# Moving a weight conversion behind a neighbourhood unit's normalising products on ScalarE

## The chip, the cores and the metric

The kernel runs on one core of one Trainium2 chip. The metric is device time in microseconds (us) of one execution; the median over the runs shown is compared. A profiled execution stands beside it, with its own time and with its span, which is the time from the first to the last instruction of the program. Engines are called TensorE (PE in the profile, PEld for its weight loads), VectorE (DVE), ScalarE (ACT), GpSimd (POOL) and SyncE (SP).

## The reference, cut to what matters

Two layers of a hybrid encoder on 512 tokens of width 1024. In each layer one projection feeds three mixers, which are merged by gates; a SwiGLU FFN and a gated input embedding follow. The mixer that the change touches is the 2-D neighbourhood attention: 8 heads, each query row sees a window of 8 x 16 neighbours, with a relative bias.

```python
proj = h @ w_in[i]
qa, ka, va, glu_in, qc, kc, vc, gates = jnp.split(proj, SPLITS, axis=-1)
ya = diff_attention(qa, ka, va, ...)
yb = conformer_conv(glu_in, ...)
yc = neighbourhood_attention(qc, kc, vc, rpb[i])
...
# neighbourhood_attention, one grid row at a time
s = jnp.einsum('bhwd,bhrwcd->bhwrc', q_r, kn).astype(jnp.float32) * scale
s = s + bias.transpose(0, 2, 1, 3)[None].astype(jnp.float32)
a = jax.nn.softmax(s.reshape(B, HC, GRID_W, KR * NA_KC), axis=-1)
...
return jnp.einsum('bhwrc,bhrwcd->bhwd', a, vn)
```

## The kernel before, in words

Activations lie transposed: 128 channels on the partitions, 512 tokens along the free dimension. Each float32 operand is held as two parts, a high one (rounded by a copy on ScalarE) and a low one (the rest, by a subtraction on VectorE), and a product is three matmuls on TensorE (`mm3`): high weights by high input, high weights by low input, low weights by high input. So the third matmul of a block is the first that needs the low part of the weights.

A block of weights of 128 x 1024 goes through `weights` (L189): a DMA into `wr`, a conversion on ScalarE into `wh` (the line of the helper is L145), and the subtraction on VectorE into `wl` (L159). Each of the three tags has 3 buffers. A block takes 24 matmuls (8 chunks of 3), and after every fourth chunk `tick` may put other work into the order of TensorE.

The order on TensorE is the order in which the program emits. The order on the other engines is made by a scheduler from priorities; the conversions of weights are put ahead by 400 places (`w_ahead`), so a conversion stands early in ScalarE's order, as soon as its buffers are free. `behind(i, then)` forces instruction `i` to stand after `then` in the order of their engine, with no wait beyond that.

A neighbourhood unit (`natten_unit`) is one head. There are 8 in a layer, called unit 0 to unit 7 here. Its first part emits the score matmuls for two halves (tiles `b` and `e`), a reduce with the bias added (L738, VectorE), four exponentials with their sums (ScalarE), a reciprocal for each half (L744, VectorE) and four normalising products on ScalarE (a copy with a scale, two for each half). Three ticks later TensorE transposes the four tiles (L754) and the result is split into `pt`, and two ticks after that the products with the values follow (L764).

The blocks of weights and the score matmuls of the units come in this order on TensorE in each layer. Q and K are the query and key blocks of neighbourhood pair 1 to 3, G and U the last gate and value blocks of the convolution's input, dQ and dK those of the differential attention's heads. dV is that mixer's value block; it is made by `values`, which converts on its own and does not go through `weights`.

| block on TensorE | units whose scores come in it or at its end |
|---|---|
| Q1 | unit 0 at its end |
| K1 | unit 1 at its end |
| G, Q2 | none (unit 0 is transposed in G, unit 1 in Q2) |
| K2 | unit 2 in its middle |
| U | unit 3 in its middle |
| Q3 | none |
| K3 | unit 4 in its middle |
| dQ0 | unit 5 in its middle |
| dK0 | none |
| dV | unit 6 in its middle, unit 7 at its end |
| dQ1, dK1, gatec 0 | none (unit 6 is transposed in dQ1, unit 7 in dK1) |

In the profile the conversions run in the order of the program. The name of a conversion tells the phase alone, so the blocks are told apart by counting: in layer 0 the conversions at 72.26, 77.47, 83.84, 91.16, 98.41 and 106.13 us are those of G, Q2, K2, U, Q3 and K3, and those at 155.79 and 156.74 us are dK1 and gatec 0.

A list `first_come` orders conversions already: `urgent` (for the splits of the transposed tiles) enters a count of 3, every call of `weights` takes one from each count in `gives_way`, and at zero the conversion of that call is put behind the entered split.

Of the kernel before, what the change touches and what calls it, by code (L numbers as in the profile page):

```python
# [14 lines left out]
AF = mybir.ActivationFunctionType  # L15
# [37 lines left out]
ORDER = (0, 2, 4, 6, 1, 3, 5, 7)  # L53
GAP = 144
AHEAD = 3
BACC = dict(dynamic_dma_scratch_size=1024)


# [4 lines left out]
class Net:  # L63
# [107 lines left out]
    def urgent(self, low):  # L171

        self.first_come.append([AHEAD, self.high, low])

    def gives_way(self, low):

        for u in self.first_come:
            u[0] -= 1
            if not u[0]:
                self.behind(self.high, u[1])  # L180
                self.behind(low, u[2])
        self.first_come = [u for u in self.first_come if u[0]]

    def weights(self, ap, n, then=None):
# [530 lines left out]
    def natten_unit(self, pr, u, st4, k2, st, y):  # L715

        nc, i = self.nc, self.i
        mm = nc.tensor.matmul
        head = 2 * pr + u
        bs = [self.sb(t, [P, 2, NW]) for t in ("b", "e")]  # L720
        with self.tc.high_priority(offset=100):
            for half, b in enumerate(bs):
                nc.sync.dma_start(b, self.a["bias"][i, head, half])
        m = self.sb("s", [P, 8])
        es = []
        for half, b in enumerate(bs):
            sc = self.ps("sc", (P, 2, NW))
            for t in range(2):
                qt = 2 * half + t
                keys = (lambda a, qt=qt: a[:, qt * P - P:qt * P + P]) if qt else \  # L730
                    (lambda a: a.rearrange("p (a b) -> p a b", b=P)[:, 0::3])
                self.scores(sc[:, t] if qt else sc[:, t].rearrange("p (a b) -> p a b", b=P),
                            st4, k2, u, slice(qt * P, (qt + 1) * P), keys, t == 0,
                            skip_group_check=True)
            for t in range(2):
                qt = 2 * half + t
                es.append(b[:, t])
                nc.vector.tensor_tensor_reduce(  # L738
                    out=b[:, t], in0=sc[:, t], in1=b[:, t], scale=-1.0, scalar=3.0e38,
                    op0=ALU.add, op1=ALU.min, accum_out=m[:, qt:qt + 1])  # L740
                self.act(b[:, t], b[:, t], AF.Exp, table="exp", scale=-1.0, bias=m[:, qt:qt + 1],
                         accum_out=m[:, 4 + qt:5 + qt])
            c = slice(4 + 2 * half, 6 + 2 * half)
            nc.vector.reciprocal(m[:, c], m[:, c])  # L744
            for t in range(2):
                self.act(b[:, t], b[:, t], AF.Copy, scale=m[:, c][:, t:t + 1])
        yield 3
        ps = []
        for half in range(2):
            pt = self.ps("tr", (P, 4, P))  # L750
            for n in range(4):
                kc, q = 2 * half + n // 2, (2 * half + (n + 1) // 2) % 4
                c = (kc != q - 1 if q else kc == 3) * P
                nc.tensor.transpose(pt[:, n], es[q][:, c:c + P], self.ident)  # L754
            pp = self.sb("pt", [P, 2, 512], F32R)
            self.urgent(self.split(pp[:, 0], pp[:, 1], pt.rearrange("p a b -> p (a b)")))
            ps.append(pp)
        yield 2
        av = self.ps(("av", "mm")[u])
        hc = (pr % 2) * 256 + u * P  # L760
        vs = st[pr // 2]
        for kc, (o, n, c) in enumerate(((0, 192, MOVE), (MOVE, 256, 256), (192, 256, 0), (320, 192, 256))):
            for k in range(2):
                mm(av[:, o:o + n], vs[kc // 2][:, kc % 2, hc:hc + P], ps[kc // 2][:, k, c:c + n],  # L764
                   start=kc == k == 0, stop=kc == 3 and k == 1, skip_group_check=True)
        rs, ro = (slice(0, 64), slice(64, P))[::-1 if u else 1]
        self.split(y[rs, 0], y[rs, 1], av[rs])
        self.tt(y[rs, 1], y[rs, 1].bitcast(F32), av[ro], ALU.add)
# [781 lines left out]
```

## Time and profile before

| | us |
|---|---|
| median of 3 runs | 1757.81 |
| lowest and highest | 1756.70 and 1757.99 |
| time of the profiled execution | 1756.33 |
| its span | 1754.6 |
| ScalarE busy | 965.5 |
| VectorE busy | 1427.1 |

The units of layer 0 lie at about 77 to 175 us of the span, those of layer 1 at about 946 to 1044 us. In the timeline each row has the start in us, the duration in us, the engine, the line, the operation with out<-in, and the count of instructions merged into the row; in brackets stands the idle time ahead of it and what ended it. On ScalarE and VectorE the next instruction starts about 0.1 us ahead of the end of the last.

### The profile page before, as it was taken

What the parts mean: (1) busy time and instruction counts of PE and PEld (TensorE: products, weight loads), DVE (VectorE), ACT (ScalarE), POOL (GpSimd) and SP (SyncE); (2) the same over time, 40 slices, a digit from 0 to 9 for tenths busy, and PEclk for the clock granted to TensorE, in tenths of its full rate; (3) what the DMA queues carried; (4) which work ended last, traced back from release to release, by engine and by line L of the source; (5) the groups of instructions that cost most, each with busy time, mean ns of one, the idle gap of its engine ahead of it and who ended that gap; (6) DMA issues with size and microseconds to landing.
All of it is one profiled execution on the core that took longest, in us unless ns stands there. A gap on an engine that the chain in (4) does not pass through costs nothing.

```text
span 1754.6 us, 24852 instructions
## 1 busy us (share of the span) xinstructions
PE 1747.0 (100%) x8842; PEld 1484.2 (85%) x8842; DVE 1427.1 (81%) x2371; ACT 965.5 (55%) x1737; POOL 104.0 (6%) x114
## 2 busy tenths in 40 slices
PE   9999999999999999999999999999999999999998
PEld 7888888888888888888888888888888988888887
DVE  7968987998799687797776789889887985977876
ACT  5576545226577275574545665553365763745654
POOL 0000000000121020100000000000001210201000
PEclk9999999999999999999999999999999999999999
DMA  6575641334757365543545755323256774755332
GB/s 227 162 193 157 165 123 49 108 99 141 232 160 185 120 169 157 143 120 127 158 130 165 202 141 158 105 73 96 93 178 197 184 171 121 181 143 155 96 107 95
DMA packets 114636, 253.81 MB, mean 145 GB/s; under 512 B 16848, under 2 KB 23504, under 8 KB 114512
## 3 DMA queue, kind: packets, MB, share of 16 engines
q1 hardware_dynamic: 101264, 228.10, 42.8%
q0 software_dynamic: 12672, 23.07, 7.9%
q8 instruction: 70, 1.15, 0.3%
q10 hardware_dynamic: 576, 1.05, 0.2%
q14 instruction: 54, 0.44, 0.1%
HBM read 215.46 MB, written 7.34 MB: 127 GB/s over the span
## 4 chain that ended last, share of the span: by engine, by line
PE 94%; DVE 2%; ACT 1%; DMA 1%; issue 1%; SPq 0%; POOL 0%; ACTq 0%; POOLq 0%; DVEq 0%
PE ffn_mm L1032 6%; PE ffn_sc L1032 6%; PE ffn_mm L196 4%; PE ffn_mm L197 4%; PE ffn_mm L198 4%; PE ffn_mm L1035 3%; PE ffn_sc L1035 3%; PE mergea_mm L198 2%; PE mergea_mm L196 2%; PE mergea_mm L197 2%; PE ffn_tr L1032 2%; PE diff_sc L819 2%; PE gatec_mm L197 2%; PE gatec_mm L196 2%; PE gatec_mm L198 2%; PE gateb_mm L198 2%
## 5 line engine op out<-in xcount | busy, mean ns | idle before, releaser
L162 DVE SCALAR_TENSOR_TENSOR conv_z<-glu_z,pre_par,conv_z 128x512 f32<-128x512 f32 x240 | 179.5, 748 | 3.4
L145 ACT ACTIVATE ffn_wh<-ffn_wr 128x1024 fp32r<-128x1024 f32 (+1 forms) x92 | 92.8, 1021 | 99.4 <-PE ffn_mm L197 70.0
L159 DVE TENSOR_TENSOR ffn_wl<-ffn_wr,ffn_wh 128x1024 fp32r<-128x1024 f32 (+1 forms) x92 | 107.1, 1175 | 21.0 <-ACT ffn_wh L145 20.5
L998 POOL DMA_DIRECT2D ffn_qk<-w_fu x88 | 78.0, 994 | 588.5 <-DMA ffn_qk<-w_fu 329.5
L145 ACT ACTIVATE mergea_wh<-mergea_wr 128x1024 fp32r<-128x1024 f32 (+1 forms) x32 | 27.1, 846 | 96.8 <-PE mergea_mm L197 79.6
L159 DVE TENSOR_TENSOR ffn_t<-ffn_mm,wo_rb 128x512 f32<-128x512 f32 (+1 forms) x46 | 31.1, 677 | 51.7 <-PE ffn_mm L198 51.7
L159 DVE TENSOR_TENSOR ffn_wl<-ffn_qk,ffn_wh 128x1024 fp32r<-128x1024 f32 x44 | 53.6, 1218 | 11.0 <-ACT ffn_wh L145 10.9
L145 ACT ACTIVATE diff_a<-diff_sc,diff_s 128x512 f32<-128x512 f32 x32 | 22.0, 689 | 72.9 <-DVE diff_s L912 72.9
L145 ACT ACTIVATE ffn_wh<-ffn_qk 128x1024 fp32r<-128x1024 f32 x44 | 46.7, 1062 | 26.8 <-PE ffn_mm L197 16.2
L196 PE MATMUL ffn_mm<-ffn_v,ffn_wh 128*128 128x512 f32 x132 | 51.4, 389 | 0.0
L197 PE MATMUL ffn_mm<-ffn_v,ffn_wh 128*128 128x512 f32 x132 | 51.4, 389 | 0.0
L198 PE MATMUL ffn_mm<-ffn_v,ffn_wl 128*128 128x512 f32 x132 | 51.3, 389 | 0.0
L196 PE MATMUL ffn_mm<-ffn_y,ffn_wh 128*128 128x512 f32 x132 | 51.3, 389 | 0.0
L197 PE MATMUL ffn_mm<-ffn_y,ffn_wh 128*128 128x512 f32 x132 | 51.3, 389 | 0.0
L198 PE MATMUL ffn_mm<-ffn_y,ffn_wl 128*128 128x512 f32 x132 | 51.3, 389 | 0.0
L145 ACT ACTIVATE natten_wh<-natten_wr 128x1024 fp32r<-128x1024 f32 x24 | 25.4, 1057 | 42.2 <-issue 15.2
L1032 PE MATMUL ffn_sc<-wo_h,ffn_wh 128*128 128x512 f32 x176 | 48.0, 394 | 0.0
L159 DVE TENSOR_TENSOR ffn_t<-ffn_t,ffn_e 128x256 f32<-128x256 f32 x84 | 46.2, 550 | 1.0 <-ACT ffn_e L145 0.9
L912 DVE TENSOR_REDUCE diff_s<-diff_sc 128x1 f32<-128x512 f32 x64 | 42.3, 683 | 3.7 <-PE diff_sc L819 3.6
L1032 PE MATMUL ffn_mm<-wo_h,ffn_wh 128*128 128x512 f32 x160 | 43.6, 394 | 0.0
L242 POOL TENSOR_TENSOR diff_rc<-diff_sm,pre_power 128x4 f32<-128x4 f32 x8 | 8.9, 1115 | 560.6 <-DVE diff_sm L162 560.6
L159 DVE TENSOR_TENSOR ffn_t<-ffn_t,ffn_t 128x512 f32<-128x512 f32 x44 | 30.2, 686 | 11.5 <-ACT ffn_t L145 11.5
(904 smaller groups left out, 5988.5 us busy)
## 6 DMA issues: line engine op xcount, KB each, us to landing
ffn_qk<-w_fu POOLq DMA_DIRECT2D x88, 256.0 KB, 6.7
ffn_wr<-w_fg SPq DMA_DIRECT2D x44, 512.0 KB, 4.2
ffn_wr<-w_fd SPq DMA_DIRECT2D x32, 448.0 KB, 4.0
ffn_r<-w_fu SPq DMA_DIRECT2D x44, 256.0 KB, 3.1
ffn_qk<-w_fg SPq DMA_DIRECT2D x44, 256.0 KB, 3.2
ffn_qk<-w_fu SPq DMA_DIRECT2D x44, 256.0 KB, 3.2
natten_wr<-w_in SPq DMA_DIRECT2D x16, 512.0 KB, 4.1
diff_wr<-w_in SPq DMA_DIRECT2D x16, 512.0 KB, 4.0
```

What stands on the lines that cost most here:

```text
L145: i = self.nc.scalar.activation(out, in_, func, **kw)
L159: return self.nc.vector.tensor_tensor(out, a, b, op)
L162: return self.nc.vector.scalar_tensor_tensor(out, a, s, b, op0, op1)
L196: mm(out, wh, ah, start=first, stop=False, **kw)
L197: mm(out, wh, al, start=False, stop=False, **kw)
L198: mm(out, wl, ah, start=False, stop=last, **kw)
L242: nc.gpsimd.tensor_tensor(col, ms, self.power, ALU.pow)
L819: self.nc.tensor.matmul(out, st4[:, u, qs], keys(st), start=first and n == 0, stop=n == 1, **kw)
L912: nc.vector.tensor_reduce(out=m[:, u:u + 1], in_=sc, op=ALU.max, axis=AX.X, negate=True)
L998: nc.gpsimd.dma_start(q, wu[:, lo], accum_op=ALU.add)
L1032: mm(out, wh[:, c], bs[k][b], start=first and k == 0, stop=False, skip_group_check=True)
L1035: mm(out[:, 0], wl[:, c], bs[k][b][:, 0], start=False, stop=k == 3, skip_group_check=True)
```

## The change

After the two normalising products of each half, the last of them is entered in `first_come` with a count of 2 and no partner on VectorE. So the conversion on ScalarE of the second call of `weights` that follows a unit is put behind the last normalising products of both halves of that unit. Nothing is computed otherwise, and no instruction is added or removed.

```diff
+ROWS_AHEAD = 2
...
             if not u[0]:
                 self.behind(self.high, u[1])
-                self.behind(low, u[2])
+                if u[2] is not None:
+                    self.behind(low, u[2])
...
             nc.vector.reciprocal(m[:, c], m[:, c])
             for t in range(2):
-                self.act(b[:, t], b[:, t], AF.Copy, scale=m[:, c][:, t:t + 1])
+                last = self.act(b[:, t], b[:, t], AF.Copy, scale=m[:, c][:, t:t + 1])
+            self.first_come.append([ROWS_AHEAD, last, None])
         yield 3
```

## The prediction

> **What bounds the kernel now.** I read the page first, parts 1 and 2, then the waits of TensorE, then its timeline and ScalarE's around the units.
>
> ```profile
> span 1754.6 us, 24852 instructions
> PE 1747.0 (100%) x8842; PEld 1484.2 (85%) x8842; DVE 1427.1 (81%) x2371; ACT 965.5 (55%) x1737; POOL 104.0 (6%) x114
> PEclk9999999999999999999999999999999999999999
> ```
>
> TensorE is busy all the time at a full granted clock. [...] So the room is in the waits, and there is hardly any:
>
> ```profile
> PE pre_av L348 <- DVE pre_zeror L421: 1.1, 1, 1.1
> PE natten_tr L754 <- ACT natten_e L145: 0.5, 2, 0.3
> ```
>
> The columns are total us, times, longest. The first is the start of the kernel. The second is what the change can touch: twice, once in each layer, the transposes of unit 6 wait for a normalising product. Matmul ends are modelled, so the loss is larger than the 0.5 us and is read from the starts (timeline of TensorE: unit 1's eight transposes undisturbed, then unit 6's in layer 0 and layer 1):
>
> ```profile
> 94.82 0.49 PE L754 MATMUL natten_tr<-pre_ident,natten_b 128*128 128x128 f32 x3
> ...
> 95.61 0.48 PE L196 MATMUL natten_mm<-glu_h,natten_wh 128*128 128x512 f32 x1
> ...
> 159.12 0.49 PE L754 MATMUL natten_tr<-pre_ident,natten_b 128*128 128x128 f32 x3
> 159.90 0.84 PE L754 MATMUL natten_tr<-pre_ident,natten_e 128*128 128x128 f32 x4 [0.29 <-ACT natten_e L145]
> ...
> 160.60 0.48 PE L196 MATMUL diff_mm<-glu_h,diff_wh 128*128 128x512 f32 x1
> ...
> 1027.90 0.49 PE L754 MATMUL natten_tr<-pre_ident,natten_b 128*128 128x128 f32 x3
> ...
> 1029.28 0.48 PE L196 MATMUL diff_mm<-ple_h,diff_wh 128*128 128x512 f32 x1
> ```
>
> Undisturbed they take 95.61 - 94.82 = 0.79 us; here 1.48 and 1.38 us. The loss is 0.69 + 0.59 = 1.28 us. That is all that this change can win on TensorE.
>
> **What the change moves.** It adds no instruction. But its count of 2 does not only reach the late unit. The second block behind units 0 to 4 is G, Q2, Q3, K3 and dK0; behind unit 5 it is dQ1; behind units 6 and 7 it is dK1, for both. A conversion now runs when its buffer comes free, two blocks ahead of its use, which is often before the unit's scores exist. After the change it waits for the unit's whole chain of reduce, exponentials, reciprocal and products. And since conversions keep the order of the program among themselves, the ones behind it (K2 behind Q2, gatec 0 behind dK1, dV behind dK0) move with it. The price is set by one comparison for each unit: the low part of the weights must be there when the block's third matmul (L198) is due.
>
> The step from the last product to that low part, from the rows of dK1 now (ScalarE, then VectorE):
>
> ```profile
> 155.79 1.04 ACT L145 ACTIVATE diff_wh<-diff_wr 128x1024 fp32r<-128x1024 f32 x1
> 156.74 1.05 ACT L145 ACTIVATE gatec_wh<-gatec_wr 128x1024 fp32r<-128x1024 f32 x1
> ...
> 163.40 0.90 ACT L145 ACTIVATE natten_e<-natten_e,natten_s 128x256 f32<-128x256 f32 x2
> ```
> ```profile
> 156.87 1.23 DVE L159 TENSOR_TENSOR diff_wl<-diff_wr,diff_wh 128x1024 fp32r<-128x1024 f32 x1 [0.82 <-ACT diff_wh L145]
> ```
>
> The conversion starts 0.10 us before the end of the one ahead (the 155.79 row ends at 156.83, the next starts at 156.74), takes 1.05, and the low part starts 0.04 us later and takes 1.23: 2.22 us from the end of the last product. One conversion that leaves the way shortens a chain behind it by its 0.95 us (156.74 - 155.79).
>
> *Units 6 and 7 to dK1, layer 0.* Now both conversions, dK1 and gatec 0, stand in the middle of unit 6's chain and delay units 6 and 7 by 2 x 0.95 = 1.90 us. Unit 7's last product ends at 164.30; with both gone, at 162.40. The low part of dK1 is ready at 164.62. dK1's third matmul is due at:
>
> ```profile
> 163.90 0.39 PE L198 MATMUL diff_mm<-glu_h,diff_wl 128*128 128x512 f32 x1
> ```
>
> So 164.62 - 163.90 = +0.72 us, net: that due time holds the 0.69 us of waiting that goes away, so TensorE really waits 1.41 us there and gets 0.69 back. The wait for unit 6 is replaced by a wait for dK1, with a longer one.
>
> *Unit 0 to G and unit 1 to Q2, layer 0.*
>
> ```profile
> 72.26 1.06 ACT L145 ACTIVATE glu_wh<-glu_wr 128x1024 fp32r<-128x1024 f32 x1 [0.34 <-PE natten_sc L705]
> ...
> 77.47 1.06 ACT L145 ACTIVATE natten_wh<-natten_wr 128x1024 fp32r<-128x1024 f32 x1 [1.06 <-PE natten_mm L197]
> ...
> 82.79 0.91 ACT L145 ACTIVATE natten_e<-natten_e,natten_s 128x256 f32<-128x256 f32 x2 [0.23 <-DVE natten_s L744]
> 83.84 1.06 ACT L145 ACTIVATE natten_wh<-natten_wr 128x1024 fp32r<-128x1024 f32 x1
> ...
> 89.31 0.90 ACT L145 ACTIVATE natten_e<-natten_e,natten_s 128x256 f32<-128x256 f32 x2
> ```
> ```profile
> 85.29 0.39 PE L198 MATMUL glu_mm<-glu_h,glu_wl 128*128 128x512 f32 x1
> ...
> 91.64 0.39 PE L198 MATMUL natten_mm<-glu_h,natten_wl 128*128 128x512 f32 x1
> ```
>
> G moves from 72.26 to behind unit 0. Q2 (77.47) leaves the front of that chain, so it ends at 83.70 - 0.95 = 82.75, G's low part at 84.97, due 85.29: hidden, with 0.32 us to spare. K2 (83.84) leaves the front of unit 1's chain: 90.21 - 0.95 + 2.22 = 91.48, due 91.64: hidden with 0.16 us.
>
> *Units 2, 3, 4 to Q3, K3, dK0.*
>
> ```profile
> 108.98 0.90 ACT L145 ACTIVATE natten_e<-natten_e,natten_s 128x256 f32<-128x256 f32 x2
> ...
> 114.11 0.90 ACT L145 ACTIVATE natten_e<-natten_e,natten_s 128x256 f32<-128x256 f32 x2
> ...
> 129.24 0.91 ACT L145 ACTIVATE natten_e<-natten_e,natten_s 128x256 f32<-128x256 f32 x2
> ```
> ```profile
> 113.58 0.39 PE L198 MATMUL natten_mm<-glu_h,natten_wl 128*128 128x512 f32 x1
> ...
> 120.82 0.39 PE L198 MATMUL natten_mm<-glu_h,natten_wl 128*128 128x512 f32 x1
> ...
> 135.57 0.39 PE L198 MATMUL diff_mm<-glu_h,diff_wl 128*128 128x512 f32 x1
> ```
>
> Even with unshortened chains the low parts come at 109.88, 115.01 and 130.15 plus 2.22, that is 112.10, 117.23 and 132.37: 1.5, 3.6 and 3.2 us ahead. These scores lie in the middle of a block, which leaves half a block more. Unit 5's chain ends before dQ1's conversion anyway. The raw blocks stay in `wr` longer, so SP's loads of later weights start later; with 3 us and more to spare in this stretch I cost that at nothing. If that cover went, the cost would be the delay of a load beyond it. No queue of POOL or SP is reordered by the change itself.
>
> *Layer 1.*
>
> ```profile
> 952.23 0.91 ACT L145 ACTIVATE natten_e<-natten_e,natten_s 128x256 f32<-128x256 f32 x2 [0.23 <-DVE natten_s L744]
> ...
> 957.73 0.90 ACT L145 ACTIVATE natten_e<-natten_e,natten_s 128x256 f32<-128x256 f32 x2
> ...
> 1032.08 0.90 ACT L145 ACTIVATE natten_e<-natten_e,natten_s 128x256 f32<-128x256 f32 x2
> ```
> ```profile
> 954.08 0.39 PE L198 MATMUL glu_mm<-ple_h,glu_wl 128*128 128x512 f32 x1
> ...
> 960.43 0.39 PE L198 MATMUL natten_mm<-ple_h,natten_wl 128*128 128x512 f32 x1
> ...
> 1032.57 0.39 PE L198 MATMUL diff_mm<-ple_h,diff_wl 128*128 128x512 f32 x1
> ```
>
> The same sums: G 953.14 - 0.95 + 2.22 = 954.41, due 954.08: +0.33 (here a load of the activation table makes the chain later). Q2 958.63 + 1.27 = 959.90, due 960.43: hidden. dK1 1032.98 - 1.90 + 2.22 = 1033.30, due 1032.57: +0.73.
>
> **The sum.** 0.72 + 0.33 + 0.73 = +1.8 us. VectorE is also at work on the convolution's taps when the conversion ends, 0.75 us each:
>
> ```profile
> L162 DVE SCALAR_TENSOR_TENSOR conv_z<-glu_z,pre_par,conv_z 128x512 f32<-128x512 f32 x240 | 179.5, 748 | 3.4
> ```
>
> A tap in flight delays the low part by 0 to 0.75 us. I take about 0.25 us at each of the three tight places, an estimate between no tap and half a tap: together +2.5 us. The profiled execution took 1756.33 us, 1.5 below the median of 1757.81 and inside the runs' spread only by its lowest; the difference is added to the median: 1757.8 + 2.5 = 1760.3 us. The bounds: if everything is hidden and the old wait goes, -1.28: 1756.5. If no chain gets shorter, the terms are 0.63, 0.79 and 2.62 in layer 0 and 1.28, 0.42 and 2.63 in layer 1 (each without its 0.95 or 1.90): +8.4, 1766.2.
>
> **Rivals.** *Only the relief (1756.5 to 1758.3).* Unit 7's chain ends by 161.7 us rather than 162.4, because its reduces on VectorE no longer stand behind two subtractions of 1.23 us and ScalarE's gaps close up; dK1 is then hidden. For it: those two subtractions do go. Against: from 155.4 us on ScalarE has almost no idle time, so the chain can only shrink by what leaves it.
>
> *Slower by more than 3.5 us (about 1763.4).* One mechanism: dK1's conversion behind unit 7. If the splits of unit 6's transposes or the value copies fill the 1.90 us that the conversions leave, unit 7's product still ends at 164.30 and TensorE waits for dK1 3.3 us gross in each layer: 2.62 + 2.63 = 5.25, plus 0.33 for G, +5.6. It decides from 163.3 us on, where each layer loses 1.6. For it: the scheduler orders by its own estimate of time, and the splits stand ready there. Against: they come later in the program than unit 7.
>
> [...]
>
> *Nothing moves.* Excluded nearly: the rows show G and Q2 converted over 10 us ahead of the products that they would have to follow.
>
> *Faster by over 3.5 us* would need other idle time on TensorE; the waits show none.
>
> **How the numbers follow.** 0.2% (3.5 us) is about what a measurement of this kernel can tell from no change. The forecast (a loss of 0.5 to 3.5 us) gets 0.50, only the relief 0.16, nothing moves 0.03: within 0.2% 0.69. Slower by more 0.27, the clock 0.02: 0.29. Faster 0.02. The range runs from the relief's bound, 1756.5, to 1764.2, which holds unshortened chains at dK1 in both layers with G and a tap (5.6 + 0.8).
>
> **What would show it.** In the profile after: TensorE's wait at L754 for `natten_e` gone; dK1's conversion behind unit 7's last product and a new wait of TensorE at L198 for `diff_wl` of 1 to 2 us in each layer; G and Q2 converted at about 82.7 and 89.2 us; Q3, K3 and dK0 late and harmless. No wait at dK1, or one of 3 us, makes the sum wrong, and so does a wait at Q3, K3 or dK0.

## The result, and the profile after

The changed kernel took 1761.20 us (median of 14 runs, 1760.25 to 1762.34) against 1756.66 us (14 runs, 1755.60 to 1758.29) of the kernel before on the same chip: a ratio of 1.0025, 95% interval 1.0016 to 1.0033. It is slower by 4.5 us, just past the 0.2% that the prediction took as the least that can be told from no change. The forecast was 1760.3, that is +2.5 us on the median of 1757.81, with a range of 1756.5 to 1764.2. So the sign and the main place held and the size did not quite: the loss lies above the 0.5 to 3.5 us of the likeliest case. That the time was missed by only 0.9 us, where the loss was missed by 2.0, is luck: the median of three runs on which the forecast was built lies 1.15 us above that of all fourteen. Of the kernels further below, one execution of that of unit 0 and the profiled one of that of units 6 and 7 ran at a lower granted clock (0.85 and 0.65); their times are in the medians of the table and in no ratio.

The page of the changed kernel, its first lines and the granted clock:

```profile
span 1759.2 us, 24825 instructions
...
PE 1748.5 (99%) x8842; PEld 1483.8 (84%) x8842; DVE 1426.9 (81%) x2371; ACT 966.0 (55%) x1737; POOL 103.8 (6%) x114
...
PEclk9999999999999999999999999999999999999999
```

The same 8842 matmuls, the clock as before, and the engines' busy times within 1.5 us: only waits can have moved. The 27 instructions fewer in the page's count only wait for a semaphore (16 fewer on ScalarE, 9 on VectorE, 3 on SyncE, one more on TensorE), and none of them counts as busy. The waits of TensorE (total us, times, longest; the lines of the changed kernel stand 2 or 3 further down, so L198 and L200 are the L196 and L198 of before):

```profile
PE glu_mm L200 <- DVE glu_wl L160: 1.1, 1, 1.1
...
PE diff_mm L200 <- DVE diff_wl L160: 1.1, 2, 0.5
PE diff_mm L198 <- ACT diff_wh L146: 0.9, 2, 0.5
PE diff_sc L822 <- ACT diff_e L146: 0.3, 1, 0.3
PE diff_mm L643 <- DVE diff_v L160: 0.2, 1, 0.2
```

The wait of the transposes for `natten_e` is gone. In its place stand five others: dK1 for both parts of its weights, G for its low part, and two that the prediction did not have, the differential scores (L822) and the value product (L643).

The view measures a wait against a modelled end, so the sizes below come from starts. TensorE runs the same matmuls in the same order in both kernels, so the start of each one after the change, less its start before (both from the beginning of the span), is the loss so far. Its steps:

| place | layer 0, us | layer 1, us | forecast, both layers |
|---|---|---|---|
| beginning of the span, up to 147 us | -0.16 | | none |
| dV, the first value block | +0.31 | +0.47 | 0 |
| unit 6's old wait | -0.70 | -0.58 | -1.28 |
| dK1, gross | +1.54 | +1.54 | +2.73, with taps +3.2 |
| differential scores | +0.40 | +0.60 | 0 |
| G | 0 | +1.36 | +0.33, with a tap +0.6 |
| **at the last matmul** | | **+4.72** | **+2.5** |

The places sum to +4.78; the rest of -0.06 is spread over the span.

*dK1 in layer 0*, in the timelines of TensorE, ScalarE and VectorE of the changed kernel:

```profile
159.26 0.49 PE L757 MATMUL natten_tr<-pre_ident,natten_b 128*128 128x128 f32 x3
...
160.06 0.48 PE L198 MATMUL diff_mm<-glu_h,diff_wh 128*128 128x512 f32 x1
...
162.65 0.39 PE L200 MATMUL diff_mm<-glu_h,diff_wl 128*128 128x512 f32 x1
163.49 0.50 PE L198 MATMUL diff_mm<-glu_h,diff_wh 128*128 128x512 f32 x1 [0.45 <-ACT diff_wh L146]
163.82 0.40 PE L199 MATMUL diff_mm<-glu_h,diff_wh 128*128 128x512 f32 x1
164.74 0.50 PE L200 MATMUL diff_mm<-glu_h,diff_wl 128*128 128x512 f32 x1 [0.53 <-DVE diff_wl L160]
```
```profile
161.59 0.90 ACT L146 ACTIVATE natten_e<-natten_e,natten_s 128x256 f32<-128x256 f32 x2
162.38 1.05 ACT L146 ACTIVATE diff_wh<-diff_wr 128x1024 fp32r<-128x1024 f32 x1
```
```profile
163.47 1.22 DVE L160 TENSOR_TENSOR diff_wl<-diff_wr,diff_wh 128x1024 fp32r<-128x1024 f32 x1 [2.38 <-ACT diff_wh L146]
```

Unit 6's eight transposes take 160.06 - 159.26 = 0.80 us, undisturbed. The block ahead ends at 162.65, and dK1's first matmul would start 0.23 us later, the step of undisturbed ones (91.19, 91.42, 91.64 us in the kernel before). But unit 7's last product ends at 162.49, its conversion runs from 162.38, the low part from 163.47 to 164.69, and the third matmul starts at 164.74. That is the chain of the prediction, step by step; VectorE was idle for 2.38 us ahead of the low part, so no tap stood in its way here.

*G in layer 1* (TensorE, ScalarE, VectorE of the changed kernel):

```profile
955.22 0.40 PE L199 MATMUL glu_mm<-ple_h,glu_wh 128*128 128x512 f32 x1
956.68 0.50 PE L200 MATMUL glu_mm<-ple_h,glu_wl 128*128 128x512 f32 x1 [1.06 <-DVE glu_wl L160]
```
```profile
952.84 0.91 ACT L146 ACTIVATE natten_e<-natten_e,natten_s 128x256 f32<-128x256 f32 x2 [0.23 <-DVE natten_s L746]
953.65 1.04 ACT L146 ACTIVATE glu_wh<-glu_wr 128x1024 fp32r<-128x1024 f32 x1
```
```profile
954.71 0.42 DVE L740 CUSTOM_DVE_ANT_0 natten_b<-natten_sc,natten_b 128x256 f32<-128x256 f32 x1 [1.90 <-PE natten_sc L822]
...
955.05 0.42 DVE L740 CUSTOM_DVE_ANT_0 natten_b<-natten_sc,natten_b 128x256 f32<-128x256 f32 x1
...
955.40 1.22 DVE L160 TENSOR_TENSOR glu_wl<-glu_wr,glu_wh 128x1024 fp32r<-128x1024 f32 x1
```

The conversion ends at 954.69. VectorE then runs two reduces of unit 1 (L740), whose scores have just come, from 954.71 to 955.40, 0.69 us, and only then the low part. The order of VectorE is written into the program, and it has the two reduces first.

*The two places without a forecast.* At the differential scores TensorE writes a tile that the exponential `diff_e` on ScalarE empties, and `diff_e` follows a reduce on VectorE (`diff_s`). ScalarE in the kernel before (first fence) and in the changed one (second):

```profile
178.26 0.69 ACT L145 ACTIVATE diff_a<-diff_sc,diff_s 128x512 f32<-128x512 f32 x1 [2.24 <-DVE diff_s L912]
...
179.71 0.69 ACT L145 ACTIVATE diff_e<-diff_sc,diff_s 128x512 f32<-128x512 f32 x1 [0.67 <-DVE diff_s L912]
```
```profile
180.82 0.69 ACT L146 ACTIVATE diff_a<-diff_sc,diff_s 128x512 f32<-128x512 f32 x1 [2.92 <-DVE diff_s L915]
...
181.50 0.62 ACT L146 ACTIVATE diff_wh<-diff_wr 128x512 fp32r<-128x512 f32 x1
...
182.54 0.68 ACT L146 ACTIVATE diff_e<-diff_sc,diff_s 128x512 f32<-128x512 f32 x1
```

VectorE there, before and after:

```profile
172.35 0.69 DVE L159 TENSOR_TENSOR diff_rp<-diff_rp,diff_r 128x512 f32<-128x512 f32 x1 [0.26 <-DMA diff_rp<-diff_rp]
...
177.54 0.68 DVE L912 TENSOR_REDUCE diff_s<-diff_sc 128x1 f32<-128x512 f32 x1
178.25 0.69 DVE L159 TENSOR_TENSOR natten_y<-natten_mm,natten_y 64x512 fp32r<-64x512 f32 x1
178.98 0.69 DVE L912 TENSOR_REDUCE diff_s<-diff_sc 128x1 f32<-128x512 f32 x1
```
```profile
174.19 0.69 DVE L160 TENSOR_TENSOR diff_rp<-diff_rp,diff_r 128x512 f32<-128x512 f32 x1 [0.94 <-DMA diff_rp<-diff_rp]
...
179.37 0.69 DVE L160 TENSOR_TENSOR natten_y<-natten_mm,natten_y 64x512 fp32r<-64x512 f32 x1
180.10 0.69 DVE L915 TENSOR_REDUCE diff_s<-diff_sc 128x1 f32<-128x512 f32 x1
...
181.54 0.69 DVE L915 TENSOR_REDUCE diff_s<-diff_sc 128x1 f32<-128x512 f32 x1
```

The two conversions of the second value block have come in between the two exponentials. That alone is little: from start to start the exponentials take 1.72 us instead of 1.45, so 0.27 more, since ScalarE was idle between them before (0.67 us). The larger part is VectorE's. `diff_a` starts 2.56 us later, where TensorE's starts stand only 0.98 us later, so it is late by 1.58 us of its own, because its reduce is. Of this, 0.86 us is there already at the subtraction for `diff_rp`, which waits for a copy by DMA, and 0.72 us is `natten_y`, which now stands ahead of the first reduce. In layer 1 the same sums give 1.99 and 0.27 us. How much was to spare is shown by the kernel of units 0 to 6 (below), which has no conversions in between: there `diff_e` is late by 1.53 us, and TensorE loses 0.1 us.

The copy lands later in a chain that can be followed in the DMA issues. The next load into `wr` is issued when the low part of dK1 has been made, at 158.12 us before and 164.72 us after. Two loads of value weights follow it, and the copies of `diff_rp` land right behind the second, the last of them at 172.23 and 174.06 us. That the later loads hold the copies back is inferred from this order; no run separates it.

At the first value block it is VectorE's order (before, then after):

```profile
148.47 0.42 DVE L159 TENSOR_TENSOR diff_v<-diff_mm,diff_v 128x256 fp32r<-128x256 f32 x1
148.92 0.42 DVE L159 TENSOR_TENSOR diff_v<-diff_v,diff_mm 128x256 fp32r<-128x256 f32 x1
```
```profile
148.38 0.42 DVE L160 TENSOR_TENSOR diff_v<-diff_mm,diff_v 128x256 fp32r<-128x256 f32 x1
148.71 0.68 DVE L160 TENSOR_TENSOR diff_rp<-diff_rp,diff_r 128x512 f32<-128x512 f32 x1
149.31 0.42 DVE L160 TENSOR_TENSOR diff_v<-diff_v,diff_mm 128x256 fp32r<-128x256 f32 x1
```

A subtraction of 0.68 us for another tile has come in between the two that empty `diff_mm`, and the second ends 0.39 us later, where TensorE's starts stand 0.16 us earlier. At both places the change names none of the instructions that moved, and none is a conversion of `weights`: the scheduler has put the instructions around the moved conversions in another order. The kernels below bear out where it matters. Of those with a count of 2 or 3 that are read by starts, the ones with this subtraction in the first pair at dV (all units, 0 to 5, 4, 0 to 6, 1 to 6) lose 0.29 us or more at L643 in each layer, and the others nothing there; the ones with the conversions between the exponentials (all units, count of 3, 7) lose 0.28 us or more at the scores in each layer, and the others at most 0.1.

### The profile page after: what moved, and what is told of

It is laid out like the page before. It is cut to its first block, busy times and chain, and to the rows that moved or that the text cites. A ratio compares the mean times of both kernels' runs of the same rounds, so it can differ in the third digit from the quotient of the medians.

```text
span 1759.2 us, 24825 instructions
## 1 busy us (share of the span) xinstructions
PE 1748.5 (99%) x8842; PEld 1483.8 (84%) x8842; DVE 1426.9 (81%) x2371; ACT 966.0 (55%) x1737; POOL 103.8 (6%) x114
## 3 DMA queue, kind: packets, MB, share of 16 engines
q8 instruction: 70, 1.15, 0.3%
q10 hardware_dynamic: 576, 1.05, 0.2%
## 4 chain that ended last, share of the span: by engine, by line
PE 95%; DVE 2%; ACT 1%; DMA 0%; issue 0%; SPq 0%; POOL 0%; POOLq 0%; ACTq 0%; DVEq 0%
PE ffn_mm L1035 6%; PE ffn_sc L1035 6%; PE ffn_mm L199 4%; PE ffn_mm L200 4%; PE ffn_mm L198 4%; PE ffn_mm L1038 3%; PE ffn_sc L1038 3%; PE mergea_mm L200 2%; PE mergea_mm L199 2%; PE mergea_mm L198 2%; PE ffn_tr L1035 2%; PE natten_mm L199 2%; PE natten_mm L198 2%; PE gateb_mm L200 2%; PE gateb_mm L199 2%; PE gateb_mm L198 2%
## 5 line engine op out<-in xcount | busy, mean ns | idle before, releaser
L198 PE MATMUL ffn_mm<-ffn_v,ffn_wh 128*128 128x512 f32 x132 | 51.4, 389 | 0.0
L200 PE MATMUL ffn_mm<-ffn_v,ffn_wl 128*128 128x512 f32 x132 | 51.3, 389 | 0.0
L198 PE MATMUL ffn_mm<-ffn_y,ffn_wh 128*128 128x512 f32 x132 | 51.3, 389 | 0.0
L200 PE MATMUL ffn_mm<-ffn_y,ffn_wl 128*128 128x512 f32 x132 | 51.3, 389 | 0.0
L146 ACT ACTIVATE natten_b<-natten_b,natten_s 128x256 f32<-128x256 f32 x64 | 30.7, 500 | 18.7 <-DVE natten_s L740 17.3
```

Of the source, the lines that this page charges most:

```text
L146: i = self.nc.scalar.activation(out, in_, func, **kw)
L198: mm(out, wh, ah, start=first, stop=False, **kw)
L200: mm(out, wl, ah, start=False, stop=last, **kw)
```

## The experiments

Theory after the result: the loss is a sum of local waits, each with its own unit: unit 0 makes G late, unit 7 makes dK1 late and turns ScalarE's order at the differential scores, the middle units turn VectorE's order at dV, and any shift away of dK1 from the middle of unit 6's chain takes the old wait away. Rival: the loss is spread over all moved conversions, since each takes its time in ScalarE's order.

All medians are compared with the kernel before on the same chip. "By starts" is the shift of the last matmul in the one profiled execution, as in the table above. It holds between -0.65 and +0.4 us from the first 12 us of the span, ahead of any unit.

| kernel: units by the new order | median, us | before, us | ratio (95%) | by starts, us |
|---|---|---|---|---|
| all (the change) | 1761.20 | 1756.66 | 1.0025 (1.0016 to 1.0033) | +4.72 |
| 6 and 7 | 1759.21 | 1756.72 | 1.0010 (1.0001 to 1.0019) | not read |
| 0 to 5 | 1757.52 | 1756.72 | 1.0004 (0.9995 to 1.0013) | +0.27 |
| 4 | 1756.14 | 1756.72 | 0.9997 (0.9988 to 1.0006) | -0.80 |
| all, count of 3 | 1758.12 | 1756.72 | 1.0007 (0.9998 to 1.0016) | +2.48 |
| 6 | 1755.18 | 1756.11 | 0.9992 (0.9984 to 1.0001) | -1.05 |
| 0 | 1759.50 | 1756.11 | 1.0014 (1.0005 to 1.0023) | +1.54 |
| 0, reduce behind G's low part | 1758.37 | 1756.11 | 1.0009 (1.0000 to 1.0018) | +1.70 |
| 7, count of 1 | 1772.27 | 1756.11 | 1.0090 (1.0077 to 1.0104) | +15.76 |
| 7 | 1758.87 | 1756.40 | 1.0014 (1.0005 to 1.0023) | +2.28 |
| 0 to 6 | 1757.69 | 1756.40 | 1.0005 (0.9997 to 1.0014) | +1.89 |
| 1 to 6 | 1755.54 | 1756.40 | 0.9994 (0.9986 to 1.0003) | +0.78 |

An interval is about 1.6 us to either side, so single rows of 1 us are not told from no change by time; there the places in the trace decide. The interval belongs to the ratio, and the ratio is not that of the two medians: in us it lies up to 0.9 below their difference (unit 0).

### The change in two halves

```diff
-            self.first_come.append([ROWS_AHEAD, last, None])
+            if head > 5:        # first kernel; "head < 6" in the second
+                self.first_come.append([ROWS_AHEAD, last, None])
```

> The entry with count 2 is made for units 6 and 7 alone. Theory (the loss is TensorE waiting for dK1 behind unit 7, plus order effects that hang on it): in each layer the wait for unit 6 goes (about -0.5 us), a wait for dK1 of 1.4 us comes, and the two conversions of the second value block stand ahead of an exponential of the differential attention, which cost 0.4 and 0.6 us in the changed kernel: together +3.0 us, ratio 1.0017. No wait at G in layer 1. Rival (the loss is spread over all conversions that lose their lead, five blocks of six in units 0 to 4): at most +1.2 us, ratio 1.0007.

> The entry with count 2 is made for units 0 to 5 alone. Theory: the wait at G in layer 1 (1.3 us) stays, and 0.2 and 0.4 us at the value block dV, whose subtractions on VectorE stand in another order; the old waits for unit 6 stay too: +1.9 us, ratio 1.0011; no wait at dK1. Rival (loss spread over all moved conversions): +3.5 us or more, ratio 1.0020, with waits at Q2, Q3, K3 or dK0 too.

Measured: +2.5 us (+0.2 to +3.3 by the interval) and +0.8 us (-0.9 to +2.3). Of the trace of units 6 and 7 only the order is read: dK1 and gatec 0 stand behind unit 7's last product, and the conversions of the second value block between the exponentials, as the theory has it. The trace of units 0 to 5 shows G in layer 1 at +1.35, dV at +0.30 and +0.45, no wait at dK1 or the scores, and, not expected, unit 6's old wait gone, -0.70 and -0.58. If both halves gain this relief (unit 6 alone and unit 7 alone do, below), the whole change gains it only once: 2.5 + 0.8 + 1.3 = 4.6, beside the 4.5 of the change; with some 1.6 us of uncertainty on each half, so close an agreement is chance. For units 0 to 5 the time excludes the rival's +3.5 us. For units 6 and 7 it holds the rival's +1.2 as well as the theory's +3.0, so that the larger part is the late units' is not shown by this pair.

### One unit alone: 6, 4 and 0

The same edit with `head == 6`, `head == 4` and `head == 0`.

> The entry with count 2 is made for unit 6 alone, not for unit 7. The order of every engine comes out as with the entries of units 6 and 7 both: once dK1 has let unit 6 pass, the scheduler puts it behind unit 7 as well. Theory: in each layer the wait for unit 6 goes (0.55 and 0.46 us between the starts), waits of 1.3 to 1.5 us at dK1 come, and 0.4 and 0.6 us at the scores behind the second value block: +2.9 us net, ratio 1.0016; the ledger of TensorE's starts shows these places and no other. Rival (loss spread over moved conversions): no wait over 0.5 us at dK1, and the time within 1 us of the kernel before.

> The entry with count 2 is made for unit 4 alone, so only dK0 is held back, and dV behind it. Theory: dK0 is in time with over 2 us to spare; what costs is that VectorE's order changes at dV, 0.2 and 0.4 us: +0.6 us, ratio 1.0003. Rival (loss spread over all moved conversions): a fifth of the change's loss or more, +0.9 us, with a wait at dK0.

> The entry with count 2 is made for unit 0 alone, so G is held back, and with it Q2 and K2 behind G. Theory: no loss at G in layer 0, where its low part is in time; 1.2 to 1.4 us in layer 1, where two reduces of unit 1 stand ahead of the low part on VectorE; nothing else: +1.3 us, ratio 1.0007. Rival (G costs by its place alone, in both layers alike): +2.4 us, ratio 1.0014.

*Unit 6.* The expectation was wrong on the order itself. ScalarE of this kernel has dK1 and gatec 0 right behind unit 6's last product and ahead of unit 7's exponentials:

```profile
157.34 0.91 ACT L146 ACTIVATE natten_e<-natten_e,natten_s 128x256 f32<-128x256 f32 x2
158.15 1.05 ACT L146 ACTIVATE diff_wh<-diff_wr 128x1024 fp32r<-128x1024 f32 x1
159.11 1.04 ACT L146 ACTIVATE gatec_wh<-gatec_wr 128x1024 fp32r<-128x1024 f32 x1
160.05 0.49 ACT L146 ACTIVATE natten_b<-natten_b,natten_s 128x256 f32<-128x256 f32 x1
```

So dK1 is in time. What was measured is what had been written down for the rival (no wait at dK1, a time within 1 us), but it does not speak for it, since dK1 does not stand behind unit 7 here. By starts it shows -0.70 at unit 6 in layer 0 and -0.58 in layer 1, nothing at any other place, and TensorE's only wait left in its view is the one at the start of the kernel. That is the whole gain the prediction counted, 0.69 + 0.59, without any price. The time agrees (-0.9 us, -2.8 to +0.2) but does not resolve it.

*Unit 4.* dK0's conversion goes late without a wait, as the prediction had it (127.92 us in place of 121.13). Yet dV shows +0.29 and +0.46 and unit 6 -0.70 and -0.58, although the edit names nothing there. At dV VectorE's order is that of the change. At unit 6 ScalarE's order has changed (this kernel, then one row of the kernel before):

```profile
155.67 0.49 ACT L146 ACTIVATE natten_e<-natten_e,natten_s 128x256 f32<-128x256 f32 x1
...
156.56 1.05 ACT L146 ACTIVATE diff_wh<-diff_wr 128x1024 fp32r<-128x1024 f32 x1
157.51 1.05 ACT L146 ACTIVATE gatec_wh<-gatec_wr 128x1024 fp32r<-128x1024 f32 x1
158.46 0.90 ACT L146 ACTIVATE natten_e<-natten_e,natten_s 128x256 f32<-128x256 f32 x2
```
```profile
159.34 0.91 ACT L145 ACTIVATE natten_e<-natten_e,natten_s 128x256 f32<-128x256 f32 x2 [0.40 <-DVE natten_s L744]
```

dK1 and gatec 0 now stand behind the last exponential of unit 6 (155.67), where in the kernel before a product and that exponential (158.09) still followed them. So the reciprocal is made while they are converted, the wait of 0.40 us for it is gone, and the last products end at 159.36 instead of 160.25 us. Units 0 to 5 have the same order there. The expected +0.6 missed the relief; measured -0.6 us (-2.1 to +1.1). The interval holds the rival's +0.9 too, but the wait at dK0 that it asks for is not there.

*Unit 0.* By starts, nothing in layer 0 and +1.35 at G in layer 1, where it stands alone. The runs lost more, 3.4 us by the medians (+0.9 to +4.0 by the interval, whose middle is +2.5): the profiled execution took 1758.09 us, which is +2.0 on the median of before, and six of the other runs lie at 1759.3 to 1760.1. What those six lost beyond G is not in the trace that was taken, and stays open; the interval does not exclude that it is the spread. Nor does the time exclude the rival's +2.4 us; that layer 0 shows nothing at G does.

### G with the reduces behind its low part

```diff
+                elif self.reduce is not None:      # in gives_way, any other call
+                    self.behind(self.reduce, low)
+                    self.reduce = None
...
+                if head == 1 and qt == 0:          # in natten_unit
+                    self.reduce = r
...
+            if head == 0:
+                self.first_come.append([ROWS_AHEAD, last, None])
```

> As with the entry for unit 0 alone, and the first reduce of unit 1 on VectorE is put behind the low part of G. Theory (two reduces ahead of the low part are what the sum lacked at G in layer 1): the wait there falls by 0.7 us, from 1.3 to about 0.6 us; +0.6 us in all, ratio 1.0003. Rival (the chain of unit 0 alone makes G late): the wait at G stays at 1.2 us or more.

G's row in the waits of TensorE in this kernel:

```profile
...
PE glu_mm L204 <- DVE glu_wl L161: 0.4, 1, 0.4
```

G's wait falls from 1.1 to 0.4 in the view, and from +1.35 to +0.68 by starts: the two reduces of 0.69 us were half of it, the late conversion is the other half. The rival, 1.2 us or more at G, is excluded. But the kernel gains nothing by starts (1.70 against 1.54), and by the runs +2.3 us (0.0 to +3.2) came where +0.6 was expected: the order around units 6 and 7 in layer 0 came out differently again, with +0.67 at unit 7's scores and +0.48 at unit 6's transposes, as large as what was saved.

### A count of 3

```diff
-ROWS_AHEAD = 2
+ROWS_AHEAD = 3
```

> The count is 3 instead of 2, for all units. Behind units 6 and 7 stands now gatec 0, behind units 0 to 5 Q2, K2, K3, dQ0, dQ1 and dK1. Theory: dK1 is in time, as in the kernel before; the wait for unit 6 goes (-1.1 us in both layers), gatec 0 is due more than 5 us later and hidden; only the exponential behind the second value block costs 0.4 to 0.6 us in each layer: -0.1 us, ratio 0.9999. Rival (any conversion that is put behind a unit costs): as the change, +4 us, ratio 1.0024.

The waits of TensorE in this kernel:

```profile
PE diff_sc L822 <- ACT diff_e L146: 1.3, 2, 0.7
```

dK1 and G no longer wait, and unit 6's relief is there (-0.67 and -0.59), as expected. The expected total of about nothing was a miss: +1.4 us (-0.4 to +2.8), +2.48 by starts, all of it at places that no block of `weights` feeds: in layer 0 +1.30 at unit 7's scores and +0.5 at a unit's product with the values, and in each layer +0.9 at the differential scores. The interval excludes the rival's +4.

### A count of 1 at unit 7

```diff
-            self.first_come.append([ROWS_AHEAD, last, None])
+            if head == 7:
+                self.first_come.append([1, last, None])
```

This holds back dQ1, the block that is due right behind unit 7's scores.

> The entry is made for unit 7 alone and with a count of 1, so dQ1, the block that TensorE needs right after unit 7's scores, waits for unit 7's last product. Theory (the loss is due time against the product's end plus 2.2 us): the product ends about 6 us after the scores, TensorE waits 7 to 8 us at dQ1 in each layer, the wait for unit 6 goes: +14.4 us, ratio 1.0082. [...] Rival (ScalarE fills the time with other work and TensorE with other matmuls): under +5 us.

TensorE in this kernel, from its timeline, and below it two stretches (busy times, counts, then the granted clock, the DMA share and GB/s):

```profile
162.57 0.80 PE L198 MATMUL diff_mm<-glu_h,diff_wh 128*128 128x512 f32 x1 [5.93 <-ACT diff_wh L146]
...
164.42 0.63 PE L198 MATMUL diff_mm<-glu_h,diff_wh 128*128 128x512 f32 x1
164.85 0.63 PE L199 MATMUL diff_mm<-glu_h,diff_wh 128*128 128x512 f32 x1
...
166.84 0.40 PE L198 MATMUL diff_mm<-glu_h,diff_wh 128*128 128x512 f32 x1
```
```profile
156.00:162.30 6.30, 0.65 (x6) 0.44 (x4) 3.22 (x14) 5.47 (x17) 0.00 (x0) 0.80 0.12 29
162.30:166.00 3.70, 3.39 (x7) 2.29 (x8) 3.45 (x3) 2.12 (x3) 0.00 (x0) 0.50 0.32 95
```

+16.2 us (+13.5 to +18.3). The price is indeed set by when the block is due: the same unit's chain ahead of a block that is due one block earlier costs 8.3 us by starts in layer 0, where with a count of 2 unit 7 alone costs 1.18 (below). And a wait of 5.93 us is followed by 3.7 us at a granted clock of 0.50: nine steps take 166.84 - 162.57 = 4.27 us, 2.2 us more than nine of 0.227 (1034.49 - 1032.45 = 2.04 us for nine in the changed kernel, at a granted clock of 1.00). The mean of 0.80 over the 6.30 us of the wait's stretch lies below the 1.00 of 150 to 156 us, so the clock was lower in a part of that stretch already. In the views of the other kernels no wait of TensorE is longer than 1.1 us; from which length on a wait costs clock was not shown. The interval holds the 14.4 us of the waits alone and excludes the rival's 5. The total came close to 14.4 because two misses cancel: the waits were 5.93 and 5.85 us where 7 to 8 were expected, and behind them the shift grew by another 2.2 and 2.6 us.

### Unit 7 alone, all but unit 7, and units 1 to 6

The same edit with `head == 7`, `head < 7` and `0 < head < 7`.

> Only unit 7 goes by the new order. In the order of the kernel that runs, dK1's and gatec 0's conversions then stand behind unit 7's last product, the second value block's two conversions stand between the two last products of the neighbourhood scores (as in the changed kernel), and everything up to the first value block is as before. Theory (the time is the sum of local waits): unit 6's old wait goes, -1.0 to -1.1 over two layers, dK1 +1.45 and +1.46, the difference scores +0.4 to +0.6 in each layer; together about +2.9 us, a ratio of 1.0016. Rival (the loss is spread evenly over all moved conversions, so one unit's share is an eighth of it): at most +1 us, 1.0006.

> Units 0 to 6 go by the new order, unit 7 by the old one; dK1's conversion then stands behind unit 6's last product and ahead of unit 7, and the second value block's conversions stand behind the last product of the scores, as before. Theory: block G in layer 1 +1.24 to +1.36, the first value block's release +0.6 over two layers, unit 6's old wait gone -1.0 to -1.1, nothing at dK1 and nothing at the difference scores; together about +0.9 us, 1.0005. Rival (spread over all moved conversions): seven eighths of the change, +3.9 us or more, 1.0022.

> As units 0 to 6, without unit 0, so that block G is converted as before. Theory: the first value block's release +0.6 over two layers, unit 6's old wait gone -1.0 to -1.1, and no wait at G, dK1 or the difference scores; together about -0.5 us, 0.9997. Rival (spread over all moved conversions): six eighths of the change, +3.4 us, 1.0019.

Measured +2.5, +1.3 and -0.9 us against +2.9, +0.9 and -0.5 of the theory and at most +1, at least +3.9 and at least +3.4 of the rival. The three intervals (+0.9 to +4.0, -0.5 to +2.5, -2.5 to +0.5) exclude the rival for the last two kernels and hold the theory in all three. The places agree. With unit 7 alone dK1 shows +1.18 and +1.09 by starts (1.45 expected), the scores +0.28 and +0.81, and unit 6 -0.70 and -0.58. Without unit 7 dK1 shows 0 and the scores 0.1 and 0. Without unit 0 as well, G shows 0. The piece that does not hold still is dV: +0.32 and +1.13 without unit 7, and in the kernel of units 1 to 6 it alone is the loss, +1.39 in layer 0 and +0.46 in layer 1. VectorE's order at dV is the same in all of these; in the two large cases it came there late. In layer 0 of units 1 to 6:

```profile
145.44 0.69 DVE L160 TENSOR_TENSOR diff_rp<-diff_rp,diff_r 128x512 f32<-128x512 f32 x1 [1.08 <-DMA diff_rp<-diff_rp]
```

The copies by DMA that this subtraction waits for landed 3.1 to 4.3 us after their issue, where they took 2.0 to 2.1 us in the same place of the changed kernel; in layer 1 of units 0 to 6 they took up to 4.3 us, and VectorE waited 0.83 us. The profiled execution of units 1 to 6 took 1756.95 us, the longest of its eleven runs, 1.4 above their median, so copies as late as these are probably rare; that they are was not shown, nor what made them late.

## Why the prediction was right, and where its size failed

**The chain at dK1: right.** Unit 7's last product was put to end at 162.40 us and ended at 162.49, with the conversion right behind it; the wait at `diff_wl` came in each layer. Gross, 1.41 and 0.73 + 0.59 = 1.32 were forecast, with 0.25 for a tap each 1.66 and 1.57; 1.54 and 1.54 were measured. The tap itself was not there in layer 0 (VectorE idle for 2.38 us); part of the 0.13 and 0.22 beyond the bare chain is the slower step behind each of two waits (below).

**The relief: right to 0.01 us**, 0.70 and 0.58 for 0.69 and 0.59. It is not bound to dK1's move behind unit 7, though: units 0 to 5, unit 4 and unit 6 alone have it too.

**Hidden at G in layer 0, Q2, Q3, K3 and dK0: right.** No row shows a wait there, though Q2 had 0.16 us to spare by the sum. In layer 0 G and Q2 were converted at 82.02 and 88.44 us, 0.7 us earlier than the 82.7 and 89.2 that were put down. TensorE did not wait for a late load (none of its waits in the view is for a DMA), and the clock did not fall in the changed kernel: 9 tenths or more in every slice of the page, and 1.00 in each of the stretches 156 to 166, 953 to 957, 1031 to 1036 and 181 to 185 us, with its waits at dK1, G and the scores. The 0.02 that the prediction gives the clock was its author's estimate; the forecast's sum does not use it. With a count of 1 at unit 7 the granted clock was 0.50 behind a wait of 5.93 us.

**G in layer 1: right in place, mis-sized.** 0.33, with a tap 0.58, was forecast and 1.36 measured. The step that failed is "the low part starts 0.04 us later": it took VectorE to be free, or behind one tap. VectorE had two reduces of unit 1 in its order ahead of the low part, 0.69 us, and putting them behind it halved the wait to 0.68. The rest of the miss is two smaller sizes: unit 0's chain got shorter by 0.74 us, not 0.95 (its last product ends at 953.75 us, with TensorE's starts 1.35 us later, against 953.14), and the step behind the wait is 0.1 us slower (957.01 - 956.68 = 0.33 us). With the 0.33 that is 1.3 of the 1.36. The timeline of VectorE before, which the prediction does not show there, has these reduces from 953.33 us on, just where the low part was now to come.

**Two terms were missing**: dV, +0.78, and the differential scores, +1.00. The prediction costed what the change moves by name, and took the order of everything else as given. It is not: at dV another instruction came in between two that empty a tile for TensorE, and at the scores VectorE's reduces came 1.6 to 2.0 us late and two conversions stood ahead of the exponential. The prediction also costed later loads at nothing, with the spare time at units 2 to 4 as the reason; at dK1, where there was none, the load behind it was issued 6.6 us later, and 0.86 us of the reduces' delay in layer 0 comes with a longer wait for copies that landed behind such loads. With unit 7 by the old order the scores show 0.1 and 0, with unit 7 alone they show +0.28 and +0.81; a unit in the middle, alone, is enough for dV. Which estimate of the scheduler tips was not shown.

**The sum.** 2.5, less 0.15 at dK1, with 0.78 at G, 0.78 at dV and 1.00 at the scores, is 4.9; by starts from 147 us on it is 4.72 + 0.16 = 4.9. By the medians the case that came true is the one of more than 3.5 us, which had 0.27, but its mechanism, the unshortened chain at dK1 (+5.6), is not what happened: both conversions' 1.90 us did go from unit 7's chain.

The best version found leaves the new order to unit 6 alone: 0.9992 (0.9984 to 1.0001) of the time before. It keeps the relief and has none of the waits, and is not told from the kernel before by its time.

## What to carry to other kernels

When a conversion is held back, compare the end of its whole chain with the moment that TensorE needs its last part, and follow that chain through every engine's written order: what stands ahead of the last link there counts as much as its duration. Follow also the load that waits for the buffer which the conversion lets go. Where a scheduler makes the order, one forced edge may turn the order of instructions that it does not name; with TensorE busy all the time, allow some 0.3 to 1 us, as in these kernels, for each place where another engine empties a tile that TensorE is about to write. Force the edge only where a wait is to be taken away, here behind one unit of eight.

## What the hardware showed that was not expected

- In the changed kernel a wait of TensorE of 0.3 to 1.1 us costs about 0.1 us more than its own length. The step from the first matmul behind it to the next is 163.82 - 163.49 = 0.33 us at dK1 in layer 0, 0.33 at G and 0.34 at the scores, where undisturbed ones follow every 0.23 (165.08 to 165.31 us); dK1, with two waits, pays it twice (165.08 - 164.74 = 0.34 us the second time).
- Copies by DMA that took 2.0 to 2.1 us to land in layer 0 of the changed kernel took 3.1 to 4.3 us in the kernel of units 1 to 6. VectorE's wait of 1.08 us for them reached TensorE: +1.39 us at dV instead of +0.31.
- With a count of 1 at unit 7, a wait of 5.93 us in layer 0 was followed by 3.7 us at a granted clock of 0.50 (162.30 to 166.00 us), 2.2 us on top of the wait; behind the waits of up to 1.1 us in the changed kernel it was 1.00 (162.30 to 166.00 and 957.00 to 960.00 us).
